# Logits of two heads at a time, with the second products at half height

## Chip, cores and metric

The kernel runs on one core of one Trainium2 chip. The metric is device time in microseconds (us), the median of several runs. The core has a matrix engine (TensorE, PE in the profile; its weight loads are listed as PEld), VectorE (DVE), ScalarE (ACT), GpSimd (POOL) and SyncE (SP, which issues the transfers). TensorE has two clock levels, 1.2 and 2.4 GHz; the profile gives the granted clock as a share of the higher one.

## What is computed

A transformer block on 2048 positions of width 1024, in float32. Its attention has two kinds of heads and an indexer that selects the keys of the second kind:

```
proj = h @ w_in                       # h: modulated RMS norm of x
# dense differential attention: 4 heads x 2 components of 64
logits = q k^T / 8 + bias(rel), causal
attn = softmax(logits_0) - lam * softmax(logits_1);  o_a = attn @ v
# indexer: 8 heads of 64, one key head
score = sum_h iw[h] * relu(iq[h] . ik), causal;  keep the 256 largest of each row
# sparse attention: 8 heads of 64 in 2 groups of 4 that share k and v
logits = q k^T / 8 + bias(rel), kept keys only;  o_b = softmax(logits) @ v
x = x + gt_a * (concat(o_a, o_b) @ w_out)
# then: RMS norm, up projection, causal width-3 convolution, silu gate, down projection
```

## The kernel before

Every float32 operand of a large product is split into two float16 parts, high and low, and a product is made of three (`acc3`, L402 to L404: high x high, high x low, low x high) or, for the logits, of two full products. Positions come in 16 blocks of 128 queries; block i sees (i + 1) x 128 keys, taken in chunks of up to 512 columns, one PSUM bank each.

For logits the contraction is only 64 long, so the 128 rows of the array carry both parts at once. In the dense attention the key tile holds the high part of component 0 in rows 0 to 63 and its low part in rows 64 to 127 (the other way round for component 1), and each query part is held twice, once in each half. L962 multiplies the high query by both key parts, L963 adds the low query times both. In the sparse attention (L1167, L1168) and in the indexer (L1042, L1043) it is the mirror image: the query tile holds high in one half of the rows and low in the other, by the parity of the head, and the key parts are each held twice; the first product uses the high keys, the second the low ones. So each chunk of each head costs two products of 128 rows into the same bank.

What then reads the bank: `logits` (L897) on VectorE, which adds bias or mask, takes the row maximum and writes to SBUF (L905, L908, L910); in the indexer ScalarE's ReLU (L1050) and VectorE's weighted sum (L1051), or VectorE alone for head 0 (L1046). The banks: `s`, shared by dense and sparse logits, has three slots in the main part (two in the first part, in which block pairs 0 and 1 are made), `si` of the indexer has two.

An attention head goes through stages: `s1` logits, row maximum, exponential (L968, L1173); `s2` the split of the weights into float16 parts and their transposing transfer (`weights_t`, tiles `hl` and `pT`); `s3` the product with the values (L989, L990, L1187, L1188); `s4` the transposed output. `pipeline` runs the stages of consecutive units side by side, one step of each in turn. A dense unit is one head of one block with both components; a sparse unit is one head of one block. The combined tile of near bias and mask (`nbm`, L1160, GpSimd) comes from a pool `nb` of five, of which the four heads' biases hold four.

The blocks go in six runs (`RUNS`): for each there are the indexer (I), the dense attention (A), the sparse attention (B and C) and the feed-forward (F, with the output projection first, O). `timeline` interleaves their steps as they are written by due times. The resulting text is not yet the order on the engines: the framework's scheduler places the instructions at build time, by their place in the text and by when operands and a free buffer are there in its own model. On the chip each engine takes its queue in that order.

One more product matters below: L760, in the setup of the bias tables, multiplies a 32 x 12 float32 matrix (`b_rb`) by 32 x 384 (`b_tmp`). It is the only one marked for another part of the array than 128 x 128.

Of the kernel before, what the change touches and what calls it, by code (L numbers as in the profile page):

```python
# [12 lines left out]
F32 = mybir.dt.float32  # L13
# [9 lines left out]
P = 128  # L23
# [58 lines left out]
def block_kernel(ctx: ExitStack, tc, x, c, w_ada, b_ada, g_attn, w_in, q_norm_a, k_norm_a, q_norm_b, k_norm_b,  # L82
# [27 lines left out]
    def stiny(name, n=1, dt=F32):  # L110
        return small.tile([P, n], dt, name=name)
# [835 lines left out]
    def a_unit(t, h, i, first, ks, vs, nb, out_, os_):  # L947
# [3 lines left out]
        def s1():  # L951
            qt = q_tile("qa", qa_s[i][:, h * 512:(h + 1) * 512])
            d["L"], d["sum"] = [], stiny("a_sum", 2)
            for cc in range(2):
                l = big(n)
                d["L"].append(l)
                mx = stiny("a_mx", 5)
                nm = 0
                for c0, c1 in chunks(n):
                    ps = s_ps(c1 - c0)  # L960
                    rhs = ks[c0 // 512][:, 0:(c1 - c0) // P, cc * P:(cc + 1) * P]
                    PE.matmul(ps, qt[:, 2 * cc], rhs, start=True, stop=False)  # L962
                    PE.matmul(ps, qt[:, 2 * cc + 1], rhs, start=False, stop=True)  # L963
                    nm = logits(ps, l, c0, c1, n, nb, None, mx, nm)
                    yield (c1 - c0) / 960 + 0.15
                m = stiny("a_m")
                V.tensor_scalar(mx[:, :nm], mx[:, :nm], ga_neg, None, op0=ALU.mult, op1=ALU.min, accum_out=m)
                S.activation(l[:, :n], l[:, :n], AF.Exp, scale=ga_inv, bias=m, accum_out=d["sum"][:, cc:cc + 1])  # L968
# [49 lines left out]
    def att_i(b0, nb_):  # L1018

        t = b0 // 4  # L1020
        for b1 in range(max(b0, 2), b0 + nb_, 2):
# [8 lines left out]
            for c in range(t + 1):  # L1030
                ki = X.tile([P, 4, 256], F16, name="ki", bufs=BUFS["ki"])
                nc.sync.dma_start(ki, ki_s[c])
                for j, i in enumerate(blks):
                    n = (i + 1) * P
                    sc_, qi = scs[j], qis[j]
                    c0, c1 = c * 512, min(c * 512 + 512, n)
                    if c1 <= c0:
                        continue
                    kk = ki[:, 0:(c1 - c0) // P]
                    for h in range(8):  # L1040
                        ps = s_ps(c1 - c0, "si")
# [103 lines left out]
    def b_unit(t, g, b, r, ks, vs, nb, st):  # L1145
        i = 4 * t + b
        n = (i + 1) * P
        d = {}

        def s1():  # L1150
            if r == 0:
# [5 lines left out]
            near = nb  # L1157
            if i >= 2:
                near = nb_tile("nbm")
                G.tensor_tensor(near, nb, st["m"][:, n - 256:n], op=ALU.add)  # L1160
            l = d["l"] = big(n)
            mx = stiny("b_mx", 5)
            nm = 0
            for c0, c1 in chunks(n):
                ps = s_ps(c1 - c0)
# [5 lines left out]
            m = d["m"] = stiny("b_m", 3)  # L1171
            V.tensor_scalar(mx[:, :nm], mx[:, :nm], gb_neg, None, op0=ALU.mult, op1=ALU.min, accum_out=m[:, 0:1])  # L1172
            S.activation(l[:, :n], l[:, :n], AF.Exp, scale=gb_inv, bias=m[:, 0:1], accum_out=m[:, 1:2])  # L1173

        def s2():
            yield from weights_t(d, i, d["l"], 2.0 ** PB)

        def s3():
            m = d["m"]
            V.reciprocal(m[:, 2:3], m[:, 1:2])  # L1180
            po = s_ps(512, "o")

            def pv(pp, b0, b1):
                for j in range(b0, b1):
                    v = vs[j // 4][:, j % 4]
                    hi, lo = pp[:, j - b0], pp[:, b1 - 2 * b0 + j]
                    PE.matmul(po[:, 0:128], hi, v[:, 0:128], start=(j == 0), stop=False)  # L1187
                    PE.matmul(po[:, 0:64], lo, v[:, 0:64], start=False, stop=(j == i))  # L1188

            yield from weights_v(d, pv)  # L1190
            tmp = X.tile([P, 64], F32, name="obt", bufs=2)
            S.activation(tmp, po[:, 64:128], AF.Copy, scale=m[:, 2:3])
            V.scalar_tensor_tensor(st["o"][:, r], po[:, 0:64], m[:, 2:3], tmp, op0=ALU.mult, op1=ALU.add)

        def s4():
            pt = s_ps(512)
# [5 lines left out]
                              ot.rearrange("p k l q -> p k (l q)"))  # L1202
            yield 0.5

        return [s1(), s2(), s3(), s4()] if r == 3 else [s1(), s2(), s3()]


    x1_s = [[dram.tile([TT, D], F32, name=f"x1_s{t}_{v}") for v in range(2)] for t in range(NT)]
# [281 lines left out]
```

## Time and profile before

| | |
|---|---|
| median of 3 runs | 3229.09 us (3227.54 to 3232.38) |
| profiled execution | 3229.96 us, its span 3228.3 us |
| TensorE busy | 2823.8 us, 87% |
| VectorE busy | 2543.7 us, 79% |
| ScalarE busy | 2008.1 us, 62% |
| GpSimd busy | 1227.3 us, 38% |
| mean granted TensorE clock | 0.951 |

The busy time of an engine counts its instructions' intervals, overlaps once. Matmuls are pipelined: an interval runs from its start to a modelled end, and the next one starts before it. In a list of groups, "idle before" is the time the engine stood idle just ahead of them, and the names after "<-" say what ended it; "issue" means that nothing in the trace explains it. In a timeline each row gives start, duration, engine, line, operation, out<-in, and the part of the array used (rows*columns), then the size of output and type.

### The profile page before, as it was taken

How to read it: one execution, taken by the hardware profiler on the slowest of the kernel's cores; microseconds unless marked ns; L12 is line 12 of the kernel's file. 1: busy time of each engine (PE TensorE's matmuls, PEld its weight loads, DVE VectorE, ACT ScalarE, POOL GpSimd, SP SyncE). 2: the span in 40 equal slices, each digit the busy share in tenths (PEclk: the TensorE clock that was granted, in tenths of full speed). 3: DMA queues.
4: the chain of work that ended last, by engine and by line, in shares of the span. 5: the costliest groups of instructions: out<-in, count | busy, mean ns of one | idle time of the engine just before them, and what ended most of it. 6: DMA issues, size and time to landing. Idle time of an engine off the chain costs nothing. (4 is left out here: it accounts for less than half of the span.)

```text
span 3228.3 us, 53238 instructions
## 1 busy us (share of the span) xinstructions
PE 2823.8 (87%) x17571; PEld 1624.0 (50%) x17571; DVE 2543.7 (79%) x6659; ACT 2008.1 (62%) x3645; POOL 1227.3 (38%) x1493
## 2 busy tenths in 40 slices
PE   5799896986899898978898999789899898888899
PEld 3345453543666475644444544444444445656476
DVE  8766888887988999977999898796788967977222
ACT  5977654563755675778555975567746678556133
POOL 2100354220656275502650660006516602845155
PEclk9999897998899899989999999889999998999899
DMA  9798875426887779996458879964685598799776
GB/s 352 240 361 301 300 274 178 142 62 217 209 233 221 196 213 235 250 275 170 118 156 236 184 185 268 256 188 122 184 240 146 139 297 220 220 245 240 222 226 202
DMA packets 741142, 704.02 MB, mean 218 GB/s; under 512 B 474362, under 2 KB 583166, under 8 KB 739584
## 3 DMA queue, kind: packets, MB, share of 16 engines
q1 hardware_dynamic: 740864, 700.61, 76.5%
q8 instruction: 138, 2.26, 0.3%
q14 instruction: 140, 1.15, 0.1%
HBM read 483.24 MB, written 114.21 MB: 185 GB/s over the span
## 5 line engine op out<-in xcount | busy, mean ns | idle before, releaser
L402 PE MATMUL mm<-h2T,wu 128*128 128x256 f16 (+1 forms) x2112 | 656.2, 311 | 34.9 <-ACT ua L1287 22.0
L404 PE MATMUL mm<-h2T,wu 128*128 128x256 f16 (+1 forms) x2112 | 656.8, 311 | 0.0
L403 PE MATMUL mm<-h2T,wu 128*128 128x256 f16 (+1 forms) x2112 | 656.8, 311 | 0.0
L1089 ACT ACTIVATE cjunk<-sc,sel 128x512 bf16<-128x512 f32 (+10 forms) x281 | 395.7, 1408 | 170.1 <-DVE cjunk L1073 140.6
L1290 POOL TENSOR_SCALAR u<-ut,cws 128x256 f32<-128x256 f32 (+1 forms) x264 | 363.1, 1375 | 294.6 <-ACT ut L1285 286.7
L402 PE MATMUL mm<-wd,gT 128*128 128x512 f16 x704 | 272.1, 387 | 35.9 <-DMA wd<-wd_s 15.6
L1291 POOL TENSOR_TENSOR ua<-ua,u 128x256 f32<-128x256 f32 (+1 forms) x264 | 271.6, 1029 | 78.3 <-DVE ua L1288 60.1
L403 PEld LDWEIGHTS <-wu 128*128 128x128 f16 x2112 | 208.7, 99 | 134.0 <-issue 32.6
L403 PE MATMUL mm<-wd,gT 128*128 128x512 f16 x704 | 271.7, 386 | 0.0
L404 PE MATMUL mm<-wd,gT 128*128 128x512 f16 x704 | 271.6, 386 | 0.0
L402 PEld LDWEIGHTS <-wu 128*128 128x128 f16 x2112 | 209.0, 99 | 114.9 <-DMA wu<-wu_s 11.4
L404 PEld LDWEIGHTS <-wu 128*128 128x128 f16 x2112 | 208.9, 99 | 107.2 <-issue 1.7
L402 PE MATMUL mm<-wg,hT 128*128 128x512 f16 (+1 forms) x640 | 242.4, 379 | 16.4 <-DVE kn L487 9.6
L1288 DVE SCALAR_TENSOR_TENSOR ua<-ut,cws,ua 128x256 f32<-128x256 f32 (+1 forms) x264 | 168.4, 638 | 103.8 <-ACT ua L1287 98.5
L403 PE MATMUL mm<-wg,hT 128*128 128x512 f16 (+1 forms) x640 | 242.3, 379 | 3.5 <-DVE wg L371 3.5
L481 POOL TENSOR_TENSOR hn_r<-hn_t,mhalf 128x8 f32<-128x8 f32 (+1 forms) x64 | 97.9, 1533 | 379.2 <-DVE hn_t L479 293.9
L1000 POOL TENSOR_TENSOR a_ss<-a_ss,mhalf 128x1 f32<-128x1 f32 x64 | 46.8, 732 | 506.9 <-DVE a_ss L999 274.7
L404 PE MATMUL mm<-wg,hT 128*128 128x512 f16 (+1 forms) x640 | 236.0, 377 | 2.4 <-DVE hT L396 2.4
L1051 DVE SCALAR_TENSOR_TENSOR sc<-relu,iw_all,sc 128x512 f32<-128x512 f32 (+3 forms) x266 | 214.1, 805 | 22.0 <-ACT relu L1050 17.9
L1173 ACT ACTIVATE big<-big,b_m,gb_inv 128x128 f32<-128x128 f32 (+15 forms) x128 | 165.2, 1291 | 77.6 <-DVE b_mx L1172 77.0
L1050 ACT ACTIVATE relu<-si 128x512 f32<-128x512 f32 (+3 forms) x266 | 139.7, 538 | 116.3 <-PE si L1043 76.8
L409 DVE SCALAR_TENSOR_TENSOR hl<-big,hl 128x1024 f16<-128x1024 f32 (+7 forms) x192 | 186.8, 984 | 31.5 <-ACT hl L408 30.7
(338 smaller groups left out, 7322.1 us busy)
## 6 DMA issues: line engine op xcount, KB each, us to landing
wu<-wu_s SPq DMA_DIRECT2D x264, 512.0 KB, 4.8
wd<-wd_s SPq DMA_DIRECT2D x160, 512.0 KB, 4.8
wo<-wo_s SPq DMA_DIRECT2D x64, 512.0 KB, 5.0
wst<-in_w_ada_dram SPq DMA_DIRECT2D x22, 1024.0 KB, 10.2
wst<-in_w_up_dram SPq DMA_DIRECT2D x22, 1024.0 KB, 11.8
wu_s<-wp SPq DMA_DIRECT2D x22, 1024.0 KB, 6.4
xd<-x_s SPq DMA_DIRECT2D x64, 256.0 KB, 6.4
ka<-ka_s SPq DMA_DIRECT2D x60, 256.0 KB, 5.7
```

The costliest lines, as they stand in the source:

```text
L402: PE.matmul(ps, a(0, k), b(0, k), start=(first and k == k0), stop=False)
L403: PE.matmul(ps, a(0, k), b(1, k), start=False, stop=False)
L404: PE.matmul(ps, a(1, k), b(0, k), start=False, stop=(last and k == k0 + nk - 1))
L409: V.scalar_tensor_tensor(lo, src, scale, hi, op0=ALU.mult, op1=ALU.subtract)
L481: G.tensor_tensor(r[:, :nh], t[:, :nh], mhalf[:, :nh], op=ALU.pow)
L1050: S.activation(r, ps, AF.Relu)
L1051: V.scalar_tensor_tensor(sc_[:, c0:c1], r, w, sc_[:, c0:c1], op0=ALU.mult, op1=ALU.add)
L1089: S.activation(junk[:, :ns[j]], scs[j][:, :ns[j]], AF.Sign, bias=C[:, j:j + 1].bitcast(F32), accum_out=cnt[:, j:j + 1])
L1173: S.activation(l[:, :n], l[:, :n], AF.Exp, scale=gb_inv, bias=m[:, 0:1], accum_out=m[:, 1:2])
L1288: V.scalar_tensor_tensor(a, ut[:, 1:n + 1], cws[:, 1, cc:cc + 1], a, op0=ALU.mult, op1=ALU.add)
L1290: G.tensor_scalar(u0, ut[:, 0:n], cws[:, 0, cc:cc + 1], None, op0=ALU.mult)
L1291: G.tensor_tensor(a, a, u0, op=ALU.add)
```

## The change

In all three places two heads (or the two components of a dense head) go together. Two banks are taken, both first products are written, then both second products, then the two evictions. Each second product uses 64 rows only: rows 0 to 63 for the first of the two and 64 to 127 for the other. What falls away is the product of the two low parts. In the built program these 944 second products are marked 64 x 128, at row 0 or row 64, and so are their weight loads; every other one stays at 128 x 128, but for L760 at 32 x 32. In the sparse attention a unit is now two heads: `s1` interleaves their chunks and makes both exponentials at its end, `s2` and `s3` take the two heads one after the other. Pools keep their sizes, and the numbers of products and evictions stay.

```diff
@@ a_unit, s1 (dense)
+            for c0, c1 in chunks(n):
+                pss = [s_ps(c1 - c0), s_ps(c1 - c0)]
+                kc = ks[c0 // 512][:, 0:(c1 - c0) // P]
+                for cc in range(2):
+                    PE.matmul(pss[cc], qt[:, 2 * cc], kc[:, :, cc * P:(cc + 1) * P], start=True, stop=False)
+                for cc in range(2):
+                    rs = slice(64 * cc, 64 * cc + 64)
+                    PE.matmul(pss[cc], qt[rs, 2 * cc + 1], kc[rs, :, cc * P:(cc + 1) * P], start=False, stop=True)
+                for cc in range(2):
+                    nms[cc] = logits(pss[cc], d["L"][cc], c0, c1, n, nb, None, mxs[cc], nms[cc])
                     yield (c1 - c0) / 960 + 0.15
@@ att_i (indexer)
+                    pss = []
                     for h in range(8):
-                        ps = s_ps(c1 - c0, "si")
-                        PE.matmul(ps, qi[:, h], kk[:, :, 0:P], start=True, stop=False)
-                        PE.matmul(ps, qi[:, h], kk[:, :, P:2 * P], start=False, stop=True)
+                        if h % 2 == 0:
+                            pss = [s_ps(c1 - c0, "si"), s_ps(c1 - c0, "si")]
+                            for e in range(2):
+                                PE.matmul(pss[e], qi[:, h + e], kk[:, :, 0:P], start=True, stop=False)
+                            for e in range(2):
+                                rs = slice(64 * e, 64 * e + 64)
+                                PE.matmul(pss[e], qi[rs, h + e], kk[rs, :, P:2 * P], start=False, stop=True)
+                        ps = pss[h % 2]
@@ b_units, b_unit (sparse)
-                for r in range(4):
-                    yield b_unit(t, g, i % 4, r, ks, vs, nbs[r], st)
+                for r in range(0, 4, 2):
+                    yield b_unit(t, g, i % 4, r, ks, vs, nbs[r:r + 2], st)
...
             for c0, c1 in chunks(n):
-                ps = s_ps(c1 - c0)
+                pss = [s_ps(c1 - c0), s_ps(c1 - c0)]
                 kk = ks[c0 // 512][:, 0:(c1 - c0) // P]
-                PE.matmul(ps, st["q"][:, r], kk[:, :, 0:P], start=True, stop=False)
-                PE.matmul(ps, st["q"][:, r], kk[:, :, P:2 * P], start=False, stop=True)
-                nm = logits(ps, l, c0, c1, n, near, st.get("m"), mx, nm)
-                yield (c1 - c0) / 960 + 0.15
+                for e in range(2):
+                    PE.matmul(pss[e], st["q"][:, r0 + e], kk[:, :, 0:P], start=True, stop=False)
+                for e in range(2):
+                    rs = slice(64 * e, 64 * e + 64)
+                    PE.matmul(pss[e], st["q"][rs, r0 + e], kk[rs, :, P:2 * P], start=False, stop=True)
+                for e in range(2):
+                    nms[e] = logits(pss[e], d[e]["l"], c0, c1, n, nears[e], st.get("m"), mxs[e], nms[e])
+                    yield (c1 - c0) / 960 + 0.15
```

The second products are L965, L1053 and L1185 in the changed kernel, the first ones L962, L1050 and L1182. Two places of TensorE's queue follow, both in the sparse attention of block 12, group 0, whose query tile is qb_26922 in both programs; s_ is a bank of logits, kb_ a chunk of keys, si_ a bank of the indexer, mm_ one of the feed-forward's down projection. First the start of the first head, before:

```order
L1167 LDWEIGHTS qb_26922
L1167 MATMUL s_26931<-kb_26898,qb_26922 128x512
L1168 LDWEIGHTS qb_26922
L1168 MATMUL s_26931<-kb_26898,qb_26922 128x512
L1167 LDWEIGHTS qb_26922
L1167 MATMUL s_26935<-kb_26900,qb_26922 128x512
L1168 LDWEIGHTS qb_26922
L1168 MATMUL s_26935<-kb_26900,qb_26922 128x512
```

The same place in the changed program:

```order
L1182 LDWEIGHTS qb_26922
L1182 MATMUL s_26935<-kb_26898,qb_26922 128x512
L1182 LDWEIGHTS qb_26922
L1182 MATMUL s_26936<-kb_26898,qb_26922 128x512
L1185 LDWEIGHTS qb_26922
L1185 MATMUL s_26935<-kb_26898,qb_26922 128x512
L1185 LDWEIGHTS qb_26922
L1185 MATMUL s_26936<-kb_26898,qb_26922 128x512
```

Where the first head's two chunks stood, the first chunk of two heads stands, and its second products are neighbours. Second, the first chunk of the third head, before:

```order
L1167 LDWEIGHTS qb_26922
L1167 MATMUL s_27149<-kb_26898,qb_26922 128x512
L1168 LDWEIGHTS qb_26922
L1168 MATMUL s_27149<-kb_26898,qb_26922 128x512
L404 LDWEIGHTS gT_25429
L404 MATMUL mm_27125<-wd_27153,gT_25429 128x512
L402 LDWEIGHTS gT_25274
L402 MATMUL mm_27126<-wd_27153,gT_25274 128x512
L1042 LDWEIGHTS qi_24384
L1042 MATMUL si_24657<-ki_24387,qi_24384 128x512
L1043 LDWEIGHTS qi_24384
L1043 MATMUL si_24657<-ki_24387,qi_24384 128x512
```

The same stretch in the changed program, where the first chunk of the fourth head (s_27089) and the second chunk of the third (s_27162) are made:

```order
L1050 LDWEIGHTS qi_24389
L1050 MATMUL si_24577<-ki_24392,qi_24389 128x512
L1053 LDWEIGHTS qi_24389
L1053 MATMUL si_24577<-ki_24392,qi_24389 128x512
L1182 LDWEIGHTS qb_26922
L1182 MATMUL s_27089<-kb_26898,qb_26922 128x512
L1185 LDWEIGHTS qb_26922
L1185 MATMUL s_27089<-kb_26898,qb_26922 128x512
L1182 LDWEIGHTS qb_26922
L1182 MATMUL s_27162<-kb_26900,qb_26922 128x512
L1185 LDWEIGHTS qb_26922
L1185 MATMUL s_27162<-kb_26900,qb_26922 128x512
```

Here each second product stands behind its own first product, as before, and has products of full height on both sides. Of the 472 pairs of second products 110 stand next to each other as in the first place; in the other 362 something stands between the two, mostly as in the second one.

## Rows read from the trace of the kernel before

**Rows 1.** The page: busy us (share of the span) of each engine.
```profile
PE 2823.8 (87%) x17571; PEld 1624.0 (50%) x17571; DVE 2543.7 (79%) x6659; ACT 2008.1 (62%) x3645; POOL 1227.3 (38%) x1493
```

**Rows 2.** Stretches: us, busy of PE, PEld, DVE, ACT, POOL; clock, DMA share, GB/s.
```profile
600.00:1000.00 400.00, 331.01 (x2169) 207.94 (x2168) 341.84 (x1147) 239.43 (x602) 157.56 (x221) 0.93 0.61 170
1000.00:1400.00 400.00, 360.00 (x2642) 237.81 (x2640) 371.04 (x1138) 261.41 (x556) 187.22 (x271) 0.97 0.85 230
1400.00:1600.00 200.00, 164.22 (x885) 82.42 (x884) 161.93 (x459) 140.99 (x241) 66.56 (x66) 0.91 0.68 182
1600.00:2000.00 400.00, 375.94 (x2218) 190.18 (x2217) 356.74 (x879) 275.74 (x452) 173.70 (x178) 0.99 0.79 200
2000.00:2200.00 200.00, 163.08 (x965) 83.65 (x963) 167.24 (x448) 115.58 (x185) 21.78 (x29) 0.90 0.84 214
2200.00:2800.00 600.00, 549.39 (x3309) 295.56 (x3308) 475.15 (x1082) 416.85 (x602) 259.90 (x294) 0.97 0.74 199
2800.00:3000.00 200.00, 169.67 (x1427) 114.20 (x1427) 142.05 (x354) 106.23 (x173) 101.66 (x133) 0.95 1.00 237
```

**Rows 3.** Timeline of TensorE: logits in a dense stretch.
```profile
2000.97 0.38 PE L1042 MATMUL si<-ki,qi 128*128 128x512 f16 x1
2001.18 0.38 PE L1043 MATMUL si<-ki,qi 128*128 128x512 f16 x1
...
2001.62 0.38 PE L1168 MATMUL s<-kb,qb 128*128 128x512 f16 x1
```

**Rows 4.** Groups: the second products; xcount | busy us, mean ns | idle before.
```profile
L963 PE MATMUL s<-ka,qa 128*128 128x512 f16 (+3 forms) x320 | 116.5, 369 | 0.0
...
L1168 PE MATMUL s<-kb,qb 128*128 128x512 f16 (+3 forms) x320 | 111.2, 353 | 0.0
L1043 PE MATMUL si<-ki,qi 128*128 128x512 f16 (+3 forms) x304 | 108.9, 359 | 0.0
```

**Rows 5.** Timeline of TensorE: a float32 transpose, then around L760.
```profile
125.47 0.38 PE L403 MATMUL mm<-wg,hT 128*128 128x512 f16 x1
...
125.68 0.38 PE L392 MATMUL tp<-idf,xt 128*128 128x128 f32 x2
...
128.20 0.38 PE L404 MATMUL mm<-wg,hT 128*128 128x512 f16 x1
128.51 0.49 PE L760 MATMUL pb<-b_tmp,b_rb 32*12 32x384 f32 x1
...
128.84 0.48 PE L760 MATMUL pb<-b_tmp,b_rb 32*12 32x384 f32 x1
129.25 0.39 PE L402 MATMUL mm<-wg,hT 128*128 128x512 f16 x1
129.48 0.38 PE L403 MATMUL mm<-wg,hT 128*128 128x512 f16 x1
```

**Rows 6.** Timeline of the weight loads there; in brackets idle before and its end.
```profile
128.51 0.10 PEld L760 LDWEIGHTS pb<-b_tmp,b_rb 32*12 32x12 f32 x2 [0.42 <-issue]
129.25 0.10 PEld L402 LDWEIGHTS <-hT 128*128 128x128 f16 x1 [0.64 <-issue]
```

**Rows 7.** Busy time in 1000:1400, 1600:2000, 2200:2800 together: L963, L1043, L1168.
```profile
sum 1400.00, PE 73.81; mean PE 24.60
...
sum 1400.00, PE 67.15; mean PE 22.38
...
sum 1400.00, PE 64.38; mean PE 21.46
```

**Rows 8.** Groups: a far eviction, the sparse exponential, the combined bias tile.
```profile
L910 DVE CUSTOM_DVE_ANT_0 big<-s,mask_in 128x512 f32<-128x512 f32 (+3 forms) x256 | 147.8, 585 | 24.1 <-PE s L1168 23.9
...
L1173 ACT ACTIVATE big<-big,b_m,gb_inv 128x128 f32<-128x128 f32 (+15 forms) x128 | 165.2, 1291 | 77.6 <-DVE b_mx L1172 77.0
...
L1160 POOL TENSOR_TENSOR nbm<-nb,mask_in 128x256 f32<-128x256 f32 x112 | 95.4, 851 | 302.3 <-DVE b_mx L905 162.8 <-issue 44.7 <-DMA mask_in<-mask_s 26.1
```

**Rows 9.** The core's span and mean granted clock.
```profile
core 0: 3228.3 us, clock 0.951
```

More of the change, by code (lines that the diff above doesn't have):

```diff
@@ L953, in s1 @@
             d["L"], d["sum"] = [], stiny("a_sum", 2)
+            mxs, nms = [], [0, 0]
             for cc in range(2):
[L955 to L959, printed above, removed]
-                    ps = s_ps(c1 - c0)
[L961 to L964, printed above, removed]
+                d["L"].append(big(n))
+                mxs.append(stiny("a_mx", 5))
+            for c0, c1 in chunks(n):
[8 more added lines that the diff above has]
+                    nms[cc] = logits(pss[cc], d["L"][cc], c0, c1, n, nb, None, mxs[cc], nms[cc])
                     yield (c1 - c0) / 960 + 0.15
+            for cc in range(2):
+                l, mx, nm = d["L"][cc], mxs[cc], nms[cc]
                 m = stiny("a_m")
@@ L1143, in b_pairs, with b_unit @@
             yield None
-    def b_unit(t, g, b, r, ks, vs, nb, st):
+    def b_unit(t, g, b, r0, ks, vs, nbs, st):
         i = 4 * t + b
         n = (i + 1) * P
-        d = {}
+        d = [{}, {}]
         def s1():
-            if r == 0:
+            if r0 == 0:
                 st["q"] = q_tile("qb", qb_s[i][:, g * 512:(g + 1) * 512])
@@ L1156, in s1 @@
                     nc.sync.dma_start(st["m"][:, :n], mask_s[i])
[L1157 to L1163, printed above, removed]
+            nears, mxs, nms = [], [], [0, 0]
+            for e in range(2):
+                near = nbs[e]
+                if i >= 2:
+                    near = nb_tile("nbm")
+                    G.tensor_tensor(near, nbs[e], st["m"][:, n - 256:n], op=ALU.add)
+                nears.append(near)
+                d[e]["l"] = big(n)
+                mxs.append(stiny("b_mx", 5))
@@ L1164, in s1 @@
             for c0, c1 in chunks(n):
-                ps = s_ps(c1 - c0)
+                pss = [s_ps(c1 - c0), s_ps(c1 - c0)]
                 kk = ks[c0 // 512][:, 0:(c1 - c0) // P]
-                PE.matmul(ps, st["q"][:, r], kk[:, :, 0:P], start=True, stop=False)
-                PE.matmul(ps, st["q"][:, r], kk[:, :, P:2 * P], start=False, stop=True)
-                nm = logits(ps, l, c0, c1, n, near, st.get("m"), mx, nm)
-                yield (c1 - c0) / 960 + 0.15
-            m = d["m"] = stiny("b_m", 3)
@@ L1172, in s1 @@
-            V.tensor_scalar(mx[:, :nm], mx[:, :nm], gb_neg, None, op0=ALU.mult, op1=ALU.min, accum_out=m[:, 0:1])
-            S.activation(l[:, :n], l[:, :n], AF.Exp, scale=gb_inv, bias=m[:, 0:1], accum_out=m[:, 1:2])
+                for e in range(2):
[3 more added lines that the diff above has]
+                    PE.matmul(pss[e], st["q"][rs, r0 + e], kk[rs, :, P:2 * P], start=False, stop=True)
@@ new lines, in s1 @@
+                for e in range(2):
+                    nms[e] = logits(pss[e], d[e]["l"], c0, c1, n, nears[e], st.get("m"), mxs[e], nms[e])
+                    yield (c1 - c0) / 960 + 0.15
+            for e in range(2):
+                m = d[e]["m"] = stiny("b_m", 3)
+                V.tensor_scalar(mxs[e][:, :nms[e]], mxs[e][:, :nms[e]], gb_neg, None, op0=ALU.mult, op1=ALU.min,
+                                accum_out=m[:, 0:1])
+                S.activation(d[e]["l"][:, :n], d[e]["l"][:, :n], AF.Exp, scale=gb_inv, bias=m[:, 0:1],
+                             accum_out=m[:, 1:2])
@@ L1175, in s2 @@
         def s2():
-            yield from weights_t(d, i, d["l"], 2.0 ** PB)
+            for e in range(2):
+                yield from weights_t(d[e], i, d[e]["l"], 2.0 ** PB)
         def s3():
[L1179 to L1193, printed above, removed]
+            for e in range(2):
+                m = d[e]["m"]
+                V.reciprocal(m[:, 2:3], m[:, 1:2])
+                po = s_ps(512, "o")
+                def pv(pp, b0, b1):
+                    for j in range(b0, b1):
+                        v = vs[j // 4][:, j % 4]
+                        hi, lo = pp[:, j - b0], pp[:, b1 - 2 * b0 + j]
+                        PE.matmul(po[:, 0:128], hi, v[:, 0:128], start=(j == 0), stop=False)
+                        PE.matmul(po[:, 0:64], lo, v[:, 0:64], start=False, stop=(j == i))
+                yield from weights_v(d[e], pv)
+                tmp = X.tile([P, 64], F32, name="obt", bufs=2)
+                S.activation(tmp, po[:, 64:128], AF.Copy, scale=m[:, 2:3])
+                V.scalar_tensor_tensor(st["o"][:, r0 + e], po[:, 0:64], m[:, 2:3], tmp, op0=ALU.mult, op1=ALU.add)
@@ L1203, in s4 @@
             yield 0.5
-        return [s1(), s2(), s3(), s4()] if r == 3 else [s1(), s2(), s3()]
+        return [s1(), s2(), s3(), s4()] if r0 == 2 else [s1(), s2(), s3()]
     x1_s = [[dram.tile([TT, D], F32, name=f"x1_s{t}_{v}") for v in range(2)] for t in range(NT)]
```

## Prediction

> **What bounds the kernel now.** I read the busy times first. TensorE is busy 87% of the span and VectorE 79% [rows 1]; neither is full, so the next look is by stretch [rows 2]. Between 600 and 3000 us, where nearly all logits are made, two kinds of stretch alternate. In 1000 to 1400, 1600 to 2000 and 2200 to 2800 TensorE is busy 1285.3 of 1400 us, 92%: it is the bound there, with VectorE close behind at 86%. In 600 to 1000, 1400 to 1600, 2000 to 2200 and 2800 to 3000 it is busy 828.0 of 1000 us, 83%, and waits more for others. The busy time of one line can't be taken as its cost, since matmuls overlap in it: what one costs is its distance to the next one in a dense stretch. There a 512-column product follows the one before it after 0.217 us (2000.97 to 2001.62 in three steps), indexer and sparse logits alike [rows 3].
>
> **The change, part by part.**
>
> *Second products.* There are 320, 304 and 320 of them [rows 4]. By the causal widths they stream 8 x 136 x 128 columns in the dense attention, the same in the sparse one and 8 x 133 x 128 in the indexer, 414,720 in all, or 810 times 512 columns: 810 x 0.217 = 176 us of TensorE. If every two ran side by side, half would go, 88 us. But two can share the time of one only where they stand next to each other in TensorE's queue, and the order of the built program tells whether they do. The source writes both first products and then both second ones. The scheduler, though, places an instruction when its PSUM buffer is free, and the second buffer of a pair is often not free yet; then the second product of the first head is placed ahead of the first product of the other. In the built order 110 of the 472 pairs stand together (50 of 160 in the dense attention, 9 of 152 in the indexer, 51 of 160 in the sparse one), and 7 halves of different pairs meet in opposite rows by accident. These 110 hold 81 products of 512 columns, 15 of 384, 8 of 256 and 6 of 128: 50,048 columns, 21.2 us, and with the seven 22 us. So at most **22 us** of streaming go, not 88. Whether two halves share their time at all no row shows: the bounds are 0 and 22 us. I take 22. The Trainium skill says on the page "TensorE: Matmul & The Clock Gate", Part 3, that matmuls in distinct row groups run concurrently and start about 4 ns apart; no run here shows it, and by it the saving would be the 22 us just worked out, without it 0.
>
> *Changing the height.* The kernel before has one product that uses the array at another size than 128 rows, the bias table at L760 (32 rows, 12 columns, in two passes) [rows 5]. The full-height product ahead of it starts at 128.20 and would be followed at 128.42; L760 starts at 128.51, 0.09 us late. Its second pass starts 0.33 us after the first, so the next product was due at 129.17; it starts at 129.25, 0.08 late, and takes 0.23 to the next in place of 0.22. The weight loads, elsewhere done under the product ahead, start only then, after idle time that nothing in the trace explains ("issue") [rows 6]. So going in and out cost 0.18 us together. It isn't the type: a float32 transpose of full height starts 0.21 us after the float16 product ahead of it, without a break (125.47, 125.68). The changed program marks the 944 second products as 64 by 128. They form 819 runs in the built order (a run is one or more in a row with nothing of full height between): each is entered and left once. 819 x 0.18 = **147 us** more on TensorE. Ends: 0, if 64 rows by full width need no such break; and 0.32 us a run (262 us), if each change waited for the modelled end of the product ahead, 0.38 - 0.22 = 0.16 us [rows 3]. I take 0.18, the only measured change of size. The Trainium skill, page "TensorEngine Tiling (Array Packing)", Tiling Modes, Key Properties, states that a change of mode, not of tile, drains the engine, and its modes count 64 x 128 apart from 128 x 128; by it 0 falls away as an end and the 147 us stay as they are.
>
> Note what this makes of a pair that stays whole: at 512 columns it saves 0.217 and pays 0.18. Even 472 whole pairs would save 88 and pay 85.
>
> *Sum on TensorE*: 147 - 22 = **125 us**, 0.132 us for each second product.
>
> *How much of it reaches the end.* The three dense stretches hold 73.8, 67.2 and 64.4 us of the 116.5, 108.9 and 111.2 us that the three lines are busy, 61% [rows 4, 7]: 76 of the 125 us fall there, where TensorE idles 115 of 1400 us. I let 80% through, 61 us. The other 49 us fall where it idles 172 of 1000 us [rows 2]; waits there shrink when TensorE comes later, and I let half through, 24 us. Together **85 us**. The ends are 0 (all hidden in those 287 us) and 125.
>
> *Pairs as units, and both buffers at once.* A sparse unit now makes the logits of two heads and then two exponentials; the first exponential (1.29 us [rows 8]) comes about one head's logits later. Other parts fill that time; uncovered it counts once, at the end of the last pipeline, and is under 8 us (four evictions of 0.59 us, an exponential, its split and transposing transfer); I take 0, since the feed-forward of the run before is still queued there. The combined bias tile (GpSimd, 0.85 us, 112 of them) has five buffers with four held by the biases, so the second one of a unit waits for the first; before it waited for the head ahead just the same (162.8 us of GpSimd's idle time, at 38% busy): 0 [rows 1, 8]. The PSUM slots stay three and two; because the built order doesn't hold first products back for the partner, evictions start as before: 0. Places of the large parts (feed-forward, projections, attention) in TensorE's queue move by less than 1% of its columns over the whole program: 0, with 15 us either way kept for it. Dropping the low-by-low term changes no instruction count.
>
> **Forecast.** The profiled run took 3229.96 us for a span of 3228.3; 3229.96 + 85 = 3315, and the median shown is 0.9 us lower: **3314 us**, 2.6% slower.
>
> **Rivals.**
> 1. *No break at 64 rows, and halves side by side.* Then the 22 us of streaming go and nothing is paid; with the same shares (80% of 61%, half of 39%) 15 us reach the end: 3214 us, faster. It decides for itself below 22 / 819 = 0.027 us a run. For it: L760 differs in columns too, and no 64-row product is in the trace. Against it: both of L760's changes show the same break. If in addition the halves don't overlap, 3229.
> 2. *The break is paid but hidden.* TensorE idles 287 us between 600 and 3000, and VectorE may be the true bound in the stretches where it is above 84% [rows 2]; then 0 to 20% of the 125 us arrive, 3229 to 3254. Against it: VectorE's evictions wait 23.9 us for just these products [rows 8], so a later TensorE makes VectorE later.
> 3. *The break is dearer*, up to 0.32 us a run: 262 - 22 = 240 us, of which 68% give 3392; all of it, 3469.
> 4. *The change doesn't do what it says*: that pairs come apart is read from the built order and is in the forecast already. What is open is only whether the 117 that meet overlap; if not, the sum is 147 us and the time 3329.
>
> **Chances.** Forecast (price 0.10 to 0.25 us a run, shares 50 to 90%: 3255 to 3385) 0.60; dearer, above 3385, 0.08; hidden 0.13, of which 0.06 within 0.2% of before; no break 0.19, of which 0.04 within 0.2%. 0.2% (6.5 us) is about what a measurement of this kernel can tell from no change. So faster 0.16, same 0.10, slower 0.74. The range takes in the forecast, the hidden case, the upper half of the no-break case and part of the dearer one: 3212 to 3400; the forecast's own range is 3255 to 3385.
>
> **What would show it.** Right: from the start of a 512-column first product to the start of what follows its lone second product it is about 0.61 us (two streams and 0.18) rather than 0.43, weight loads of 64 rows start late with "issue" ahead of them, and TensorE's idle time by issue grows by some 100 us or more. In a whole pair both halves start within hundredths of a microsecond. Wrong: lone halves follow at 0.217 us (rival 1), or breaks are there but the stretches 1000 to 1400 and 1600 to 2000 are no longer (rival 2). The prediction would also fail if TensorE, with more gaps, were granted its half clock for longer than before (mean 0.951 of full [rows 9]).

## The result and the profile after

The changed kernel takes **3307.92 us** (median of 4 runs, 3301.34 to 3315.89) against 3228.56 us (4 runs, 3227.54 to 3232.38) for the kernel before: 79 us more, ratio 1.0245, 95% interval 1.0216 to 1.0274. The forecast was 3314 us, slower. Below, a "half" is a second product of 64 rows, a "run" is one or more halves in a row, and a "break" is the time lost where the height changes. The profiled execution took 3302.76 us; its span is 3301.0 us, 72.7 us more than before.

The page first: busy time, share of the span and instructions of each engine, then the core's span and mean granted clock. They answer [rows 1] and [rows 9].

```profile
PE 2969.7 (90%) x17556; PEld 1579.2 (48%) x17571; DVE 2541.8 (77%) x6659; ACT 2008.5 (61%) x3645; POOL 1215.3 (37%) x1493
...
core 0: 3301.0 us, clock 0.945
```

(The trace lacks 15 of the 17571 products, none of them a half.) VectorE, ScalarE and GpSimd have the same instructions and, within 1%, the same busy time as before. TensorE is busy 145.9 us longer (2823.8 before) and idle 73.2 us less (404.5 before, 331.3 now): half of what it got more to do is absorbed by its waits, half is the longer span. The breaks thus show as busy time, not as idle time: the rows below list a product with a modelled length of 0.38 us, and the one after it starts 0.32 us behind its start.

The stretches, in the columns of [rows 2]:

```profile
600.00:1000.00 400.00, 349.83 (x2220) 209.25 (x2219) 336.56 (x1142) 238.49 (x599) 167.66 (x234) 0.94 0.61 173
1000.00:1400.00 400.00, 381.97 (x2551) 220.58 (x2549) 341.37 (x1054) 240.51 (x519) 175.89 (x255) 0.97 0.85 227
1400.00:1600.00 200.00, 170.76 (x889) 80.74 (x887) 153.32 (x493) 150.91 (x256) 51.59 (x63) 0.84 0.67 169
1600.00:2000.00 400.00, 378.75 (x2023) 167.64 (x2022) 343.60 (x801) 253.79 (x414) 174.04 (x176) 0.98 0.71 185
2000.00:2200.00 200.00, 187.01 (x1009) 78.37 (x1006) 163.71 (x455) 110.33 (x187) 15.38 (x19) 0.87 0.90 226
2200.00:2800.00 600.00, 555.35 (x2937) 250.32 (x2936) 476.10 (x1090) 408.02 (x567) 213.16 (x227) 0.96 0.69 184
```

Read the instruction counts beside the busy time. In 2200 to 2800 TensorE is busy 555 us, 6 more than before, but finishes 2937 products where it finished 3309; in 1000 to 1400 it is 22 us busier and finishes 91 fewer. These stretches had little idle time left to give (40.0 and 50.6 us before), and less work is done in them. That the breaks alone make it so is my reading. (The later stretches also hold later work than the same stretches of before, so the counts show the lag and not only its making.)

Now the products one by one. TensorE's timeline in a dense stretch: start us, modelled length us, line, operation, tile and shape; "x2" is two neighbouring instructions of one line in one row of the list.

```profile
1700.46 0.38 PE L1050 MATMUL si<-ki,qi 128*128 128x512 f16 x1
1700.78 0.39 PE L1053 MATMUL si<-ki,qi 64*128 64x512 f16 x1
1701.09 0.23 PE L995 MATMUL o<-va,pT 128*128 128x128 f16 x1
...
1702.46 0.59 PE L962 MATMUL s<-ka,qa 128*128 128x512 f16 x2
1702.98 0.39 PE L965 MATMUL s<-ka,qa 64*128 64x512 f16 x2
1703.31 0.28 PE L994 MATMUL o<-va,pT 128*128 128x256 f16 x1
```

L1050 and L1053 are an indexer head with a **lone** second product. The half starts 0.32 us after the product ahead and the next one 0.31 us after it: 0.63 us for what takes 2 x 0.217 = 0.43 at full height [rows 3]. L962 and L965 are a pair that stayed **whole**: both first products, then both halves. From 1702.46 to 1703.31 it takes 0.85 us where four full products take 0.87. The weight loads of these places, in brackets the idle time ahead of each and what ended it, answer [rows 6]:

```profile
1700.77 0.09 PEld L1053 LDWEIGHTS <-qi 64*128 64x128 f16 x1 [0.32 <-issue]
1701.09 0.10 PEld L995 LDWEIGHTS <-pT 128*128 128x128 f16 x1 [0.23 <-issue]
...
1702.98 0.10 PEld L965 LDWEIGHTS <-qa 64*128 64x128 f16 x2 [0.42 <-issue]
1703.30 0.10 PEld L994 LDWEIGHTS <-pT 128*128 128x128 f16 x1 [0.23 <-issue]
```

The half's weights, and the weights of the full product behind it, are loaded only within 0.01 us of the product's own start, after the break. The same over the whole program, as groups (xcount | busy us, mean ns of one | idle before, and what ended it): the weight loads of the halves, the halves themselves, which answer [rows 4], and the ReLU on ScalarE that takes the indexer's logits.

```profile
L1053 PEld LDWEIGHTS <-qi 64*128 64x128 f16 x304 | 27.6, 93 | 100.3 <-issue 98.3
L965 PEld LDWEIGHTS <-qa 64*128 64x128 f16 x320 | 25.5, 94 | 97.2 <-issue 95.2
L1185 PEld LDWEIGHTS <-qb 64*128 64x128 f16 x320 | 25.0, 93 | 87.1 <-issue 85.3
...
L965 PE MATMUL s<-ka,qa 64*128 64x512 f16 (+3 forms) x320 | 105.6, 388 | 0.0
L1185 PE MATMUL s<-kb,qb 64*128 64x512 f16 (+3 forms) x320 | 95.6, 357 | 0.0
L1053 PE MATMUL si<-ki,qi 64*128 64x512 f16 (+3 forms) x304 | 109.2, 370 | 0.0
...
L1061 ACT ACTIVATE relu<-si 128x512 f32<-128x512 f32 (+3 forms) x266 | 140.5, 539 | 208.6 <-PE si L1053 149.2 <-DVE mask L1131 36.7 <-DVE sc L1062 16.2
```

A half is no shorter than a full product: 388, 357 and 370 ns on average against 369, 353 and 359 [rows 4]. The groups' busy time hardly fell (310.4 us against 336.6): few halves found their partner. And the ReLU's wait for the second product is 149.2 us; in the kernel before it was half of that:

```profile
L1050 ACT ACTIVATE relu<-si 128x512 f32<-128x512 f32 (+3 forms) x266 | 139.7, 538 | 116.3 <-PE si L1043 76.8 <-DVE sc L1051 23.0 <-DVE mask L1120 10.9
```

From the starts of all products in the trace: between two full products of 512 columns the median step is 0.216 us, from a full product to a half 0.312, from a half to a full product 0.319. So entering a run of halves costs 0.096 us, leaving it 0.103 us, **0.20 us** a run. At 128 columns the three steps are 0.056, 0.152 and 0.159 us: the price is the same, so it does not depend on the columns, while what a pair can save does. There are the 819 runs that the built order has; 117 times halves of opposite rows meet, and they start 3 or 4 ns apart; 8 times halves of the same rows meet and follow each other, in the six cases of 512 columns after 0.222 to 0.227 us.

### The profile page after: what moved, and what is told of

Its sections match the earlier page's. It is cut to its first block, busy times and chain, and to the rows that moved or that the text cites. A ratio compares the mean times of both kernels' runs of the same rounds, so it can differ in the third digit from the quotient of the medians.

```text
span 3301.0 us, 53196 instructions
## 1 busy us (share of the span) xinstructions
PE 2969.7 (90%) x17556; PEld 1579.2 (48%) x17571; DVE 2541.8 (77%) x6659; ACT 2008.5 (61%) x3645; POOL 1215.3 (37%) x1493
## 5 line engine op out<-in xcount | busy, mean ns | idle before, releaser
L1313 POOL TENSOR_SCALAR u<-ut,cws 128x256 f32<-128x256 f32 (+1 forms) x264 | 353.0, 1337 | 347.0 <-ACT ut L1308 304.2
L1314 POOL TENSOR_TENSOR ua<-ua,u 128x256 f32<-128x256 f32 (+1 forms) x264 | 263.2, 997 | 74.5 <-DVE ua L1311 53.0
L1061 ACT ACTIVATE relu<-si 128x512 f32<-128x512 f32 (+3 forms) x266 | 140.5, 539 | 208.6 <-PE si L1053 149.2
L1062 DVE SCALAR_TENSOR_TENSOR sc<-relu,iw_all,sc 128x512 f32<-128x512 f32 (+3 forms) x266 | 206.1, 775 | 52.8 <-ACT relu L1061 49.5
L408 ACT ACTIVATE hl<-big 128x1024 f16<-128x1024 f32 (+7 forms) x192 | 151.7, 803 | 104.3 <-DMA pT<-hl 92.5
```

Source lines behind the costliest of these rows:

```text
L408: S.activation(hi, src, AF.Copy, scale=scale)
L1313: G.tensor_scalar(u0, ut[:, 0:n], cws[:, 0, cc:cc + 1], None, op0=ALU.mult)
L1314: G.tensor_tensor(a, a, u0, op=ALU.add)
```

## The experiments

The theory to be tested, now with the price from the trace: each run of halves costs TensorE about 0.2 us, the order takes the pairs apart, and TensorE's added time reaches the end in part. The rivals: the sparse units or the pairing cost it; the pairs' order does; or added TensorE time is hidden. "TensorE" in the table is each kernel's runs of halves in its built order times 0.20 us, less what it saves of streaming; "shift" is its median less that of the kernel before on the same chip.

| run | what differs | TensorE | shift | ratio, 95% |
|---|---|---|---|---|
| changed kernel | | +141 | +79 | 1.0245, 1.0216 to 1.0274 |
| e1_single_half | before, second products at 64 rows | +186 | +65 | 1.0204, 1.0187 to 1.0221 |
| e2_pairs_full | changed, second products at 128 rows | 0 | +2 | 1.0011, 1.0000 to 1.0022 |
| e3_pairs_kept | changed, pairs held together | +11 | +52 | 1.0166, 1.0148 to 1.0183 |
| e4_indexer_half | before, 64 rows in the indexer only | +61 | +42 | 1.0130, 1.0110 to 1.0150 |
| e5_kept_full | e3 at 128 rows | 0 | +56 | 1.0169, 1.0147 to 1.0191 |
| e6_groups4 | halves in fours, one pool of banks | -32 | +219 | 1.0675, 1.0648 to 1.0701 |
| e7_pairs_pool5 | e3, one pool of banks | +8 | +149 | 1.0460, 1.0438 to 1.0481 |
| e8_before_pool5 | before, one pool of banks | 0 | +120 | 1.0370, 1.0337 to 1.0404 |
| e9_attention_half | before, 64 rows in the attentions only | +128 | +50 | 1.0154, 1.0128 to 1.0179 |
| e10_no_second | before, second products left out | -176 | -21 | 0.9922, 0.9900 to 0.9943 |
| e11_pairs_attention | changed, indexer at 128 rows | +85 | +26 | 1.0074, 1.0051 to 1.0097 |
| e12_half_same_order | e1 in before's queues | +185 | +66 | 1.0215, 1.0193 to 1.0238 |

**Height or pairing?** e1 changes the height alone and pairs nothing; the second product takes 64 rows, upper or lower by turns, and the source's order stays. The same edit stands at all three places:

```diff
-                    PE.matmul(ps, qt[:, 2 * cc + 1], rhs, start=False, stop=True)
+                    rs = slice(64 * cc, 64 * cc + 64)
+                    PE.matmul(ps, qt[rs, 2 * cc + 1], rhs[rs], start=False, stop=True)
```

> The kernel before, with its second products at 64 rows and nothing paired: heads one at a time, units, buffers and text order as before. The built order has 944 halves in 935 runs, and 1 us of streaming to save. Theory (each run costs one change of height in and one out, 0.20 us together as the trace of the changed kernel shows it, and some 56% of what TensorE gains in work reaches the end, 79 of 141 us): 935 x 0.20 - 1 = 186 us more on TensorE, 104 at the end: about 3333 us, slower than the changed kernel. Rival (the pairing does it: both banks taken at once, units of two heads, exponentials later): none of that is here, so about 3229.

Measured: 3292.62 us (3290.17 to 3293.36). Breaks without any pairing make the kernel slower by 65 us; the size expected was too high, since 35% of 186 us arrive and not the 56% of the changed kernel.

e2 is the changed kernel with both second products at full height, pairs and two-head units untouched:

```diff
-                                rs = slice(64 * e, 64 * e + 64)
-                                PE.matmul(pss[e], qi[rs, h + e], kk[rs, :, P:2 * P], start=False, stop=True)
+                                PE.matmul(pss[e], qi[:, h + e], kk[:, :, P:2 * P], start=False, stop=True)
```

> The changed kernel with its second products back at 128 rows: pairs, units of two heads, text order and buffers as in the changed one. Theory (height changes): no run at 64 rows, nothing saved, so 3229 give or take 15 us for the other order. Rival (pairing): as slow as the changed kernel, about 3308. If both have a part, between, and the part is read off directly.

Measured: 3229.85 us (10 runs, 3225.61 to 3238.48). Two banks at once, both sparse exponentials at the end of a unit and the new order cost nothing that can be told from no change. The loss comes with the height, or with the order that the scheduler makes for it.

But a changed program is also built in its own order. **e12** takes that away: it is e1 with the queues of all five engines held in the order of the kernel before, so that nothing but the height of 944 products and of their weight loads differs. In the trace the order on TensorE, VectorE, ScalarE and GpSimd is that of the kernel before.

```diff
+            for a, b in zip(row[:-1], row[1:]):
+                tc.add_manual_dep(MADE[b], a,
+                                  mybir.DependencyInfo(mybir.DependencyClass.NoSync, mybir.DependencyReason.DATA), reason="order")
```

> The unpaired kernel with all 944 second products at 64 rows once more, but with the queues of all five engines held in the order that the kernel before has (the build had otherwise laid them out anew for the shorter products). 930 runs, 0.7 us to save, 185 us more on TensorE: height alone, nothing else. With the order made anew it was 65 us slower. Theory (the breaks alone cost; the new order neither helps nor harms): about 65, so 3283 to 3300. Rival 1 (the new order had hidden a part): more than 80, above 3305, up to the whole 185. Rival 2 (a part of the 65 was the new order): under 50, below 3275.

Measured: 3294.37 us (3291.58 to 3297.21). This lies in the range expected: the breaks by themselves cost 66 us. The page of e12 shows them as TensorE's busy time, 173 us more than before:

```profile
PE 2997.0 (91%) x17556; PEld 1585.8 (48%) x17571; DVE 2543.1 (77%) x6659; ACT 2017.8 (61%) x3645; POOL 1222.1 (37%) x1493
```

**Would whole pairs pay?** e3 holds each second product behind its partner's first by an order edge, so that nearly all pairs stand together (478 runs of halves); e5 does the same with second products at full height (465 of the 472 pairs together).

```diff
                 for e in range(2):
-                    PE.matmul(pss[e], st["q"][:, r0 + e], kk[:, :, 0:P], start=True, stop=False)
+                    last = PE.matmul(pss[e], st["q"][:, r0 + e], kk[:, :, 0:P], start=True, stop=False)
...
-                    PE.matmul(pss[e], st["q"][rs, r0 + e], kk[rs, :, P:2 * P], start=False, stop=True)
+                    last = behind(PE.matmul(pss[e], st["q"][rs, r0 + e], kk[rs, :, P:2 * P], start=False, stop=True), last)
```

> The changed kernel, where each second product is made to stand behind the first product of its partner, so that nearly all pairs stay whole: the built order has 944 halves in 478 runs, and 85 us of streaming to save. Theory: 478 x 0.20 - 85 = 10 us more on TensorE, 6 at the end: about 3235, no faster than before, though now the pairs do run side by side. Rival (halves side by side are worth it once they are together, and the changes of height cost little): -85 us on TensorE, 48 at the end: about 3180. Rival (pairing): at or above 3308, since both banks are now waited for.

> The kernel with the pairs held together, but its second products back at 128 rows: the held order alone (465 of 472 pairs stay neighbours), no change of height, nothing saved. The held kernel was 51 us slower than before, where its work on TensorE grew by some 10 to 16 us. Theory (the held order costs the rest: the first eviction of a pair waits for the partner's bank and first product): 3229 + 35 to 45, so 3264 to 3274. Rival (the breaks cost more than their 0.20 us there, because each falls just ahead of an eviction that others wait for): 3229, within 0.3%.

Measured: e3 3279.38 us (3274.21 to 3285.04), e5 3283.20 us (3276.92 to 3284.86). The expectation of e3 missed by 44 us; e5 lies 9 us above its range and far from its rival, 3229. TensorE's sum was right, as the pages of e3 and, below it, e5 show:

```profile
PE 2849.9 (87%) x17571; PEld 1563.1 (48%) x17571; DVE 2545.4 (78%) x6659; ACT 1997.9 (61%) x3645; POOL 1203.2 (37%) x1493
```

```profile
PE 2839.1 (87%) x17571; PEld 1630.8 (50%) x17571; DVE 2539.4 (78%) x6659; ACT 1998.7 (61%) x3645; POOL 1217.6 (37%) x1493
```

TensorE is busy 26 us more than before in e3, but 15 more in e5 already, which has no half; the 11 between them are the sum. In e3 the groups of halves take about half the time of the full products before (336.6 us), since nearly every two share it:

```profile
L971 PE MATMUL s<-ka,qa 64*128 64x512 f16 (+3 forms) x320 | 62.4, 382 | 0.0
L1191 PE MATMUL s<-kb,qb 64*128 64x512 f16 (+3 forms) x320 | 60.2, 359 | 0.0
L1059 PE MATMUL si<-ki,qi 64*128 64x512 f16 (+3 forms) x304 | 57.7, 366 | 0.0
```

Their sum is 180.3 us against 310.4 in the changed kernel. e5 says where e3 lost it: with no half in the program the held order costs as much by itself. The first product of a sparse head waits longer for VectorE, in e5 and, below it, in the kernel before:

```profile
L1188 PE MATMUL s<-kb,qb 128*128 128x512 f16 (+3 forms) x320 | 107.3, 353 | 34.1 <-DVE b_mx L911 17.4 <-DVE b_mx L916 9.8 <-DVE ota L409 5.8
```

```profile
L1167 PE MATMUL s<-kb,qb 128*128 128x512 f16 (+3 forms) x320 | 112.5, 353 | 11.5 <-DVE b_mx L910 6.8 <-DVE b_mx L905 2.7 <-DMA kb<-kb_s 0.8
```

A pair that is held together needs two free banks before its second products may start, and both evictions come after them: that is how I read the longer waits for VectorE's b_mx. That the order costs 56 us is shown; how is not. In e3 this wait is 18.6 us, and ahead of the first products of all three places TensorE waits 98.6 us in e3 and 98.4 in e5 against 82.3 before, 16 us more of the 52 and 56. The granted clock is lower too, 0.943 and 0.946. Between e3 and e5 the intervals overlap: in this order whole pairs are worth nothing that can be measured, as the break-even of 0.217 against 0.20 us would have it.

**More pairs to a break.** e6 puts four halves in one run, so that a run saves twice 0.217 us; for that all logits share one pool of five banks in place of three and two. e7 is e3 with that pool, e8 the kernel before with it. The pool is this edit (the indexer then takes its bank from it too):

```diff
-    PSB = dict(mm=2, s=3, si=2, o=1)
+    PSB = dict(mm=2, s=5, o=1)
```

> Four second products in a row where there are two chunks (dense and sparse) or four heads (indexer), held together, and one pool of five banks in place of three and two (four in place of two and two in the first part). The built order has 944 halves in 276 runs and 87 us of streaming to save: 276 x 0.20 - 87 = -32 us on TensorE. Theory (work on TensorE decides, some 50% arrives): about 3213, faster than before. Rival (the held order decides: four of five banks are asked for at once, so evictions and products take turns): slower than the held pairs, above 3279.

> The kernel with the pairs held together, with one pool of five banks for all logits in place of three and two; 476 runs, 87 us of streaming to save, +8 us on TensorE. Theory (the held pairs wait for banks): with five to draw from most of the 35 to 45 us goes, 3235 to 3250. Rival (the breaks cost more than their length): as before, about 3279.

> Control for the two with five banks: the kernel before, only with one pool of five banks in place of three and two. No change of height. Both theories: 3229 within 15 us; what it differs from 3229 by is to be taken from the other two.

Measured: e6 3446.32 us (3443.37 to 3451.27), e7 3376.72 (3371.99 to 3378.28), e8 3347.55 (3336.98 to 3356.46). All three are far slower than expected, and e8, which has no half at all, already by 120 us. So the pool makes more than half of it; less that control, e7 is 29 us and e6 99 us slower, if the parts add up, which in e4 and e9 below they do not. The theories of e6 (faster) and e7 (3235 to 3250) fail, and what e6's fours cost by themselves stays open. e8's TensorE is busy 2844.1 us, 20 more than before, and idle 106 us more; its granted clock is 0.938. Its groups of the indexer's first product and of the ReLU:

```profile
L1042 PE MATMUL s<-ki,qi 128*128 128x512 f16 (+3 forms) x304 | 111.5, 370 | 95.5 <-DMA ki<-ki_s 42.9 <-DVE sc L1046 29.5 <-ACT relu L1050 12.4
...
L1050 ACT ACTIVATE relu<-s 128x512 f32<-128x512 f32 (+3 forms) x266 | 140.6, 541 | 157.7 <-DVE sc L1051 65.1 <-DVE mask L1120 37.0 <-PE s L1043 29.3
```

TensorE waits 95.5 us ahead of the indexer's first products; in the kernel before it was 35.1:

```profile
L1042 PE MATMUL si<-ki,qi 128*128 128x512 f16 (+3 forms) x304 | 108.7, 359 | 35.1 <-ACT relu L1050 17.3 <-DMA ot<-ot_s 13.0 <-DVE sc L1046 4.7
```

What ended the longer waits is the load of the keys (ki) and the indexer's own evictions. That the indexer and the attention take the banks from each other may lie behind them; these rows do not show it. Groups of four were thus not tried with the banks as they were: three and two banks don't hold four.

**How much is TensorE's time worth?** e4 and e9 split e1: halves in the indexer alone, halves in the two attentions alone (e1's edit at one place, and at the two others). e11 is the split of the changed kernel: e2's edit in the indexer alone.

> The kernel before with the second products of the indexer alone at 64 rows, unpaired: 304 halves in 304 runs, nothing saved. A third of the dose of the unpaired kernel with all three. Theory: 304 x 0.20 = 61 us more on TensorE, 34 at the end: about 3263. Rival (TensorE's gaps take up a small dose whole, and only a large one shows): within 0.2% of 3229. Rival (pairing): 3229.

> The kernel before with the second products of the dense and the sparse attention alone at 64 rows, unpaired; the indexer as before. 640 halves in 640 runs, nothing saved: 128 us more on TensorE. With all three so treated the kernel was 65 us slower, with the indexer alone 42. Theory (the place decides: the indexer's banks are two, ScalarE and VectorE wait for each product, the attention has slack): the rest of the 65, some 23 us: about 3251. Rival (the same share everywhere, 35 to 56% of the work): 45 to 72 us: 3273 to 3300.

> The changed kernel with the indexer's second products back at 128 rows. 640 halves in 531 runs, 21 us of streaming to save: 85 us more on TensorE in place of 141. Theory (the place decides, the indexer pays 42 of the changed kernel's 79 us): about 37 us slower than before or less, 3245 to 3266. Rival (the same share everywhere, 56%): 48 us, 3277.

Measured: e4 3269.75 us (3259.97 to 3272.64), e9 3273.36 (3268.11 to 3282.27), e11 3248.71 (3243.17 to 3257.34). The idea behind e9, that breaks in the indexer count nearly whole, breaks in the attentions little, and that both add up, falls: 42 and 50 us make 92, and e1 with both has 65. e11 lies in its expected range, but that range came from this idea. What the indexer's halves do is seen in its ReLU, which waits 76.8 us for the second products before, 103.5 in e4, 132.3 in e1, 138.3 in e12 and 149.2 in the changed kernel, but 70.5, 74.7 and 85.7 in e2, e11 and e9, where the indexer has none, and 73.4 in e3, where its halves stand in pairs. The group in e4 and in e11:

```profile
L1051 ACT ACTIVATE relu<-si 128x512 f32<-128x512 f32 (+3 forms) x266 | 140.7, 540 | 148.7 <-PE si L1044 103.5 <-DVE mask L1121 13.2 <-DMA ka<-ka_s 12.7
```

```profile
L1060 ACT ACTIVATE relu<-si 128x512 f32<-128x512 f32 (+3 forms) x266 | 137.9, 538 | 158.4 <-PE si L1052 74.7 <-DVE mask L1130 38.8 <-DVE sc L1061 35.8
```

The other direction is **e10**: the second products are left out of the kernel before, and with them the parts of the logits that need a low half.

```diff
-                    PE.matmul(ps, qt[:, 2 * cc], rhs, start=True, stop=False)
-                    PE.matmul(ps, qt[:, 2 * cc + 1], rhs, start=False, stop=True)
+                    PE.matmul(ps, qt[:, 2 * cc], rhs, start=True, stop=True)
```

> The kernel before without the 944 second products of the logits (the logits lack the products of the low parts, the rest is made as before): what TensorE's time is worth in the other direction. 176 us of streaming go. Theory (TensorE's work counts here by the shares seen for added work, 35 to 69%): 62 to 120 us less, 3108 to 3166, so that the 88 us of perfect pairs without any break would have been worth some 30 to 60. Rival (others bound the kernel as soon as TensorE is shorter): under 20% of it, above 3193.

Measured: 3202.49 us (3191.36 to 3204.49), ratio 0.9922: 25 us by the ratio, 21 by the medians. The time is the one of the expectation's rival, that the other engines bound the kernel. With 176 us of streaming gone, a seventh of it comes back. Its page:

```profile
PE 2701.0 (85%) x16612; PEld 1551.4 (49%) x16627; DVE 2538.3 (80%) x6659; ACT 2008.8 (63%) x3645; POOL 1214.4 (38%) x1493
...
core 0: 3189.4 us, clock 0.934
```

TensorE is busy 123 us less and the span only 39 us shorter (this execution was the shortest of the four); the others have the same work. TensorE is idle 84 us more (488.4 against 404.5), so waiting for others is the larger part. The granted clock has a part as well, 0.934 against 0.951. An estimate from these: TensorE had its half clock for (1 - 0.934) x 2 x 3189 = 421 us in place of 316, which costs at most 52 us of work, half the difference. Counted over the products that follow the one before at about twice the usual step, the time lost grows by only 11 us. At the same seventh, which is an estimate from this one dose, the 88 us that perfect pairs could save would have been worth some 12 us, even if their breaks were free.

## Why the prediction was right

- **Second products**: right. 110 whole pairs and 7 chance meetings were read from the built order; 117 meetings are in the trace. That two halves share their time no row of before showed; now the starts lie 3 or 4 ns apart. The Trainium skill ("TensorE: Matmul & The Clock Gate", Part 3) gives about 4 ns, and the trace agrees. Same rows meet 8 times and take turns. By their widths the 117 save 22 us, as taken.
- **Changing the height**: the mechanism was right, the price a little low. L760 with 32 rows gave 0.18 us [rows 5]; a 64-row run costs 0.20 (0.096 in, 0.103 out). 819 runs make 163 us in place of 147. The ends, 0 and 0.32 us a run, both fall. The Trainium skill ("TensorEngine Tiling (Array Packing)", Key Properties) has the drain at a change of mode, without a price; the trace shows one of 0.20 us.
- **Sum on TensorE**: 163 - 22 = 141 us in place of 125. TensorE's busy time grew by 145.9.
- **How much reaches the end**: mis-sized the other way. 68% was forecast; 79 of 141 us is 56%. The halves in the dense stretches hold 65.8, 64.3 and 46.8 us (L1053, L965, L1185), 57% of their groups' busy time, so their place was about as in [rows 7]. What failed is the share let through: the waits took in 73 us by the two spans, where 32% of 141 would be 45. The errors cancel, 141 x 0.56 = 79 against 125 x 0.68 = 85: that the forecast came within 6 us is in part luck. The time is nearer than the step deserves: in e12, with only the height changed, the share is 36%.
- **Pairing, units, banks, bias tile, exponentials at nothing**: right in sum; e2 puts all of them together at +2 us. The sparse exponential takes 1289 ns and waits 57.5 us (77.6 before), the combined bias tile 840 ns, as in [rows 8].
- **What whole pairs make**: save 88, pay 85 was forecast; held together they save 85 and pay 96. e3 and e5 differ by 4 us with overlapping intervals.
- **Rivals**: no break and halves that don't overlap fall by the starts in the trace. Breaks that are hidden (3229 to 3254) fall by e12. The dearer break falls by its price.
- **The signs to look for**: 0.63 us for a lone half (0.61 forecast), the late weight loads and the common start are there. "TensorE's idle time by issue" was the wrong place to look: products' modelled ends cover the break. It shows as idle time of the weight loads, 278.8 us by issue ahead of the three groups of halves (72.4 ahead of the same loads before), and as TensorE's busy time. The last sign, a longer half clock, did come in part: 0.945 against 0.951. The prediction's sum has no term for it.
- **Its sums**: two slips, on which nothing hangs. The parts of the chances add up to faster 0.15 and slower 0.75, where 0.16 and 0.74 are written. A price of 0.10 to 0.25 us with shares of 50 to 90% gives about 3259 to 3393, not 3255 to 3385.

**What stays open.** In the order of the kernel before, 36% of the breaks' time arrives (e12; 35% in e1, whose order is its own), in the changed kernel 56%. At 36% its 141 us would give some 50, so 25 to 30 us have no settled cause. They come with the halves of the indexer: the changed kernel is 55 us slower than e11 (by ratios) for 56 us more on TensorE, and its ReLU waits longest. The granted clock is a candidate too: over the span it is 0.945, before 0.951, in e12 0.948, in e11 0.954. An estimate from these, as for e10: TensorE had its half clock for 363 us, before for 316, in e11 for 298. That costs at most 23 us of work against before and 32 against e11. Counted over the products at about twice the usual step, it is 1.5 and 10.5 us more. So the clock may be much or little of it; no run holds it fixed. Nor is it known why the shares of single parts run from about 30% (e11) to 69% (e4) and do not add up; every kernel but e12 has an order of its own. Of the kernels that make all second products none beat the one before.

## What to carry to other kernels

Before two products are put side by side in the array, look up in the built queue whether they stand next to each other, and set the streaming that a pair saves (0.217 us at 512 columns, 0.109 at 256) against the way into and out of the other height (0.20 us at every width seen): a short pair, or one that the scheduler takes apart, loses. What TensorE's time is worth should be measured by leaving the work out first: here 176 us of it gave about 25 (at a lower granted clock), while 141 to 186 us added cost 65 to 79, so a saving and a cost of the same size don't weigh the same.

## What was not expected of the hardware

- The price of a change of height was nearly the same in the two sizes seen: 0.18 us with 32 rows and 12 columns (one case), 0.20 us with 64 rows at full width (819). It falls on both ways, 0.096 and 0.103 us, and is the same from 128 to 512 columns.
- Halves of 512 columns in the same rows follow each other after 0.222 to 0.227 us (six cases), so which half comes next decides between 3 ns and a whole product.
- Sharing the logits' banks among all three users, five in one pool, costs 120 us (e8), more than the breaks of e12 (66 us). I had expected nothing of it, and why it costs so much is not known beyond the waits shown.
